# Three quarters of the first MLP product as 2x2 block products with seven products of sums, in a decoder step on one core

## The chip, the core and the metric

The kernel runs on one core of one Trainium2 chip. The metric is the device time of one execution in microseconds, the median of several runs. The engines are TensorE (PE in the profile; its weight loads are PEld), VectorE (DVE), ScalarE (ACT), GpSimd (POOL) and SyncE (SP), which issues all transfers here. Each engine works through its own queue in order and waits on semaphores for the others.

## The reference

One layer of a decoder, for 512 prompt tokens and 8 new tokens (520 columns in all), d_model 1024, hidden size 4096. Two recurrent branches and their merge come first, per-layer inputs and a final norm last. What the change touches is the MLP between them:

```
hm = rms_norm(r, norm_mlp_g)
r = r + jnp.square(jax.nn.relu(hm @ w_ff1)) @ w_ff2      # w_ff1: 1024 x 4096, w_ff2: 4096 x 1024
...
hp = rms_norm(r, norm_ple_g)
r = r + jax.nn.sigmoid(hp @ w_ple_gate) * (p_l @ w_ple_proj)
```

## The kernel before

Activations lie with channels on the partitions and the 520 tokens along the free axis, so a block is 128x520. Matmuls run in a rounded 32-bit format; to keep precision, every operand is split into a high part (the value rounded, written by ACT) and a low part (the rest, a DVE subtraction), and a product is three matmuls: high weight by high activation, high by low, low by high. A matmul takes 260 columns, half of the tokens, since 520 don't fit one bank of PSUM; the result of 520 columns takes a tile `m` of two banks, of which there are two. Single banks `s` come from another pool of four.

The work with weights is a list of units. A unit is a piece of 1024x128 weights (8 tiles of 128x128) and what it multiplies: 8 x 3 x 2 = 48 matmuls (`mm`, L176). `seq` is the order in which weights are prepared. `load` brings the next piece into one of three `raw` buffers; `prep` writes its high part `wh` (ACT, L154) and its low part `wl` (DVE, L159) into one of three buffers each, and asks for the next load. `run_unit` first calls `prep` for the unit two steps ahead, then issues its matmuls, then the evaluation of its result. The order of the code is the order in each engine's queue: the schedule is written by hand.

The first MLP product has 32 units, the second 64 half units (a unit there is 8 of 32 hidden blocks). They go by halves: 16 units of the first product fill 16 hidden blocks (`ev_ff1`: on DVE the rectified product times the tokens' reciprocal root, L874, on ACT its square, L875, then high and low part, L527 and L528), and 16 units of the second product use them, two per output block, with one DVE addition per output block (`ev_ff2`, L887). The same again for the second half. The norm's gain is applied to `hm` before the product, the tokens' factor `rstd` after it.

Of the kernel before, what the change touches and what calls it, by code (L numbers as in the profile page):

```python
# [8 lines left out]
F32 = mybir.dt.float32  # L9
# [10 lines left out]
N = T + NB  # L20
# [5 lines left out]
# columns of w_in  # L26
# [10 lines left out]
class Unit:  # L37
    """One pass of weights: a [1024 or 8 tiles of 128, 128] piece and what it multiplies."""
# [7 lines left out]
def decoder_step_kernel(  # L46
# [73 lines left out]
    # ---------------------------------------------------------------- weights  # L120
    raw_of, w_of = {}, {}

    seq = []  # the units in the order in which their weights are prepared
    done = {"load": 0, "prep": 0}
    w_tags = {}

    def load():
        if done["load"] < len(seq):
            u = seq[done["load"]]
            r = rawp.tile([128, 8, 128], F32, tag="raw", name="raw")  # L130
            units[u].load(r)
            raw_of[u] = r
            done["load"] += 1

    def prep(engines=None, apart=False):
        """The next unit's weights in two parts that sum to them; a generator over the pieces,
        engines has for each the one that rounds and the one that subtracts; apart: a pause between them."""
# [4 lines left out]
        done["prep"] += 1  # L142
        r = raw_of.pop(u)
# [37 lines left out]
    def run_groups(u, lo, hi):  # L181
        """The tiles lo..hi of unit u's list; returns the evacuations that are due."""
# [15 lines left out]
    def run_unit(u):  # L198
        prep_all()
        if u in extra:  # L200
            prep_all()
        due = run_groups(u, 0, 4)
# [6 lines left out]
        w_of.pop(u)  # L209

# [3 lines left out]
    # ------------------------------------------------ phase 0: x, norms, tables  # L214
# [3 lines left out]
    og = {}  # HGRN2's outputs: the pairs 0..2; the last pair, and with it the first head's of retention  # L218
# [63 lines left out]
    def hg_near(p):  # L282
        """Scores of s == t, and of the pairs of neighbours that start at an even token."""
# [16 lines left out]
    def hg_scores(p, lvl):  # L300
        """Scores of the pairs whose level, the half size of their block, is lvl."""
# [38 lines left out]
    def hg_update(p, m):  # L340
        """From the products within blocks of m to those within blocks of 2m."""
# [40 lines left out]
    def v_dec(vT):  # L382
        """The new tokens' values by token, out to memory so that they can be read for all partitions."""
# [38 lines left out]
    def o_dec(q, Sd, psd):  # L422
        """psd rows: for each (g, half) a block of 32 rows, the last 8 of them the new tokens."""
# [8 lines left out]
    def o_ext(psd):  # L432
# [3 lines left out]
        # token 4z+l of group g: column 32(2g+z) + 24 + 4z+l of the l-th block  # L436
# [67 lines left out]
    def rsqrt(out, pieces, scale):  # L504
        """out = (x * scale + EPS) ** -0.5, x given in pieces of out"""
# [7 lines left out]
    def ones_bc(H, L, x=None):  # L513
        """The sum over partitions of H + L (+ x), on every partition: two banks of NH."""
# [58 lines left out]
    # -------------------------------------------------------- retention units  # L573
# [205 lines left out]
    # ------------------------------------------------- merge of the branches  # L779
# [53 lines left out]
    def add_squares(j, r, cs):  # L833
        """The squares of the blocks 0..6, summed, and those of block 7."""
# [28 lines left out]
    # ---------------------------------------------------------------- MLP  # L863
    def ev_ff1(i):
        def ev(ps):
            if i == 0:
                mx["hid"] = pair("X2", "hid")
                a = big.tile([128, 12, N], F32R, tag="B3", name="fa")
                b = big.tile([128, 6, N], F32R, tag="Q", name="fb")
                c = [pair(f"S{i}", "fc", F32R) for i in (0, 1, 2, 4, 5, 6, 7)]  # L870
                mx["f"] = [a[:, k] for k in range(12)] + [b[:, k] for k in range(6)] + \
                    [t[:, k] for t in c for k in range(2)]
# [3 lines left out]
            split(hidH(i % 16), hidL(i % 16), t)  # L876
# [18 lines left out]
    def ff1_half(half):  # L895
        for i in range(16):
            unit(w_ff1[0], (half * 16 + i) * 128, lambda k: mx["hmH"][:, k], lambda k: mx["hmL"][:, k],
                 ev_ff1(half * 16 + i))

    def ff2_half(half):  # L900
        w2 = w_ff2[0].rearrange("(k p) n -> p k n", p=128)
        for j in range(8):
            for z in range(2):
                k0 = half * 16 + z * 8
                src = w2[:, k0:k0 + 8, j * 128:(j + 1) * 128]
# [481 lines left out]
```

## Time and profile before

| | us |
|---|---|
| median of 3 runs | 1116.89 (1116.68 to 1117.96) |
| span of the profiled execution, first to last instruction | 1115.1 |
| PE busy in it | 1104.0 (99%) |
| DVE busy | 568.8 (51%) |
| ACT busy | 418.8 (38%) |
| POOL busy | 25.7 (2%) |
| mean granted TensorE clock | 0.998 |

A row of groups in the profile reads: line, engine, operation, tile written <- tiles read, shapes, count | busy us, mean ns of one | idle time of the engine just before them, and what ended it. A row of the timeline reads: start us, duration us, engine, line, operation, and in brackets the idle time before it with what ended it. A row of windows reads: the stretch, its length, busy us of PE, PEld, DVE, ACT and POOL with the number of instructions, the granted clock, the busy share of the DMA engines and GB/s. A row of waits reads: who waited for whom, us in total, times, the longest.

### The profile page before, as it was taken

How to read it: one execution, taken by the hardware profiler on the slowest of the kernel's cores; microseconds unless marked ns; L12 is line 12 of the kernel's file. 1: busy time of each engine (PE TensorE's matmuls, PEld its weight loads, DVE VectorE, ACT ScalarE, POOL GpSimd, SP SyncE). 2: the span in 40 equal slices, each digit the busy share in tenths (PEclk: the TensorE clock that was granted, in tenths of full speed). 3: DMA queues.
4: the chain of work that ended last, by engine and by line, in shares of the span. 5: the costliest groups of instructions: out<-in, count | busy, mean ns of one | idle time of the engine just before them, and what ended most of it. 6: DMA issues, size and time to landing. Idle time of an engine off the chain costs nothing.

```text
span 1115.1 us, 23376 instructions
## 1 busy us (share of the span) xinstructions
PE 1104.0 (99%) x10433; PEld 1085.7 (97%) x10433; DVE 568.8 (51%) x817; ACT 418.8 (38%) x621; POOL 25.7 (2%) x19
## 2 busy tenths in 40 slices
PE   8999999999999999999999999999999999999997
PEld 8999999999999999999999999999999999999997
DVE  6576767859555754442342554444222344344465
ACT  7223534343344425422322344433112433332365
POOL 1000000000011011000000000000000000000001
PEclk9999999999999999999999999999999999999999
DMA  7535252533445365433323233333333233334302
GB/s 220 152 96 171 82 172 78 156 101 115 136 139 157 114 173 155 119 95 95 95 81 108 78 96 89 104 92 95 96 96 95 76 95 95 95 92 125 88 19 78
DMA packets 231028, 123.03 MB, mean 110 GB/s; under 512 B 3960, under 2 KB 229504, under 8 KB 230800
## 3 DMA queue, kind: packets, MB, share of 16 engines
q1 hardware_dynamic: 230928, 121.54, 37.7%
q8 instruction: 82, 1.34, 0.5%
q14 instruction: 18, 0.15, 0.0%
HBM read 109.89 MB, written 11.63 MB: 109 GB/s over the span
## 4 chain that ended last, share of the span: by engine, by line
PE 98%; DVE 1%; ACT 0%; DMA 0%; issue 0%; SPq 0%; DVEq 0%
PE m L176 83%; PE m L1115 2%; PE s L1115 2%; PE s L309 1%; PE s L428 1%; PE s L489 1%; PE s L711 1%; PE s L465 1%; PE s L668 1%; PE s L491 0%; PE s L713 0%; PE s L292 0%; PE s L452 0%; PE s L404 0%; DMA xn<-in_x_prompt_dram 0%; PE s L617 0%
## 5 line engine op out<-in xcount | busy, mean ns | idle before, releaser
L159 DVE TENSOR_TENSOR wl<-raw,wh 128x1024 fp32r<-128x1024 f32 (+1 forms) x165 | 200.8, 1218 | 186.9 <-ACT wh L154 186.4
L176 PE MATMUL m<-hH,wh 128*128 128x260 f32 x1120 | 231.0, 287 | 0.0
L176 PE MATMUL m<-hH,wl 128*128 128x260 f32 x1120 | 226.0, 283 | 0.0
L176 PE MATMUL m<-hL,wh 128*128 128x260 f32 x1120 | 225.2, 283 | 0.0
L154 ACT ACTIVATE wh<-raw 128x1024 fp32r<-128x1024 f32 (+1 forms) x165 | 172.4, 1046 | 139.1 <-PE m L176 119.7
L176 PEld LDWEIGHTS m<-hH,wh 128*128 128x128 f32 x1120 | 172.3, 188 | 3.4 <-issue 1.7
L176 PEld LDWEIGHTS m<-hH,wl 128*128 128x128 f32 x1120 | 172.6, 188 | 0.0
L176 PEld LDWEIGHTS m<-hL,wh 128*128 128x128 f32 x1120 | 172.5, 188 | 0.0
L176 PE MATMUL m<-hmH,wh 128*128 128x260 f32 x512 | 103.3, 283 | 0.0
L176 PE MATMUL m<-hmH,wl 128*128 128x260 f32 x512 | 103.2, 283 | 0.0
L176 PE MATMUL m<-hmL,wh 128*128 128x260 f32 x512 | 103.0, 283 | 0.0
L176 PE MATMUL m<-fc,wh 128*128 128x260 f32 x448 | 90.1, 282 | 0.0
L176 PEld LDWEIGHTS m<-hmH,wh 128*128 128x128 f32 x512 | 79.0, 188 | 0.1
L176 PEld LDWEIGHTS m<-hmH,wl 128*128 128x128 f32 x512 | 78.9, 188 | 0.0
L176 PEld LDWEIGHTS m<-hmL,wh 128*128 128x128 f32 x512 | 78.7, 188 | 0.0
L176 PE MATMUL m<-fa,wh 128*128 128x260 f32 x384 | 77.2, 282 | 0.0
L176 PE MATMUL m<-fa,wl 128*128 128x260 f32 x384 | 77.1, 282 | 0.0
L176 PEld LDWEIGHTS m<-fc,wh 128*128 128x128 f32 x448 | 69.2, 188 | 0.0
L875 ACT ACTIVATE hid<-hid 128x520 f32<-128x520 f32 x32 | 20.4, 638 | 112.0 <-DVE hid L874 112.0
L176 PEld LDWEIGHTS m<-fa,wl 128*128 128x128 f32 x384 | 59.2, 188 | 0.0
L176 PEld LDWEIGHTS m<-fa,wh 128*128 128x128 f32 x384 | 58.9, 188 | 0.0
L874 DVE SCALAR_TENSOR_TENSOR hid<-m,x 128x520 f32<-128x520 f32 x32 | 22.4, 700 | 51.5 <-PE m L176 51.5
(321 smaller groups left out, 1662.1 us busy)
## 6 DMA issues: line engine op xcount, KB each, us to landing
raw<-in_w_in_dram SPq DMA_DIRECT2D x72, 512.0 KB, 3.9
raw<-in_w_ff_dram SPq DMA_DIRECT2D x64, 512.0 KB, 4.1
vbc<-vdd SPq DMA_DIRECT2D x16, 512.0 KB, 5.4
Sd<-in_state_hgrn_dram SPq DMA_DIRECT2D x8, 512.0 KB
out_dram<-Sd SPq DMA_DIRECT2D x8, 512.0 KB, 5.5
rSd<-in_state_ret_dram SPq DMA_DIRECT2D x8, 512.0 KB, 6.1
out_dram<-rSd SPq DMA_DIRECT2D x8, 512.0 KB
raw<-in_w_up_hg_dram SPq DMA_DIRECT2D x8, 512.0 KB, 3.9
```

What stands on the lines that cost most here:

```text
L154: S.activation(wh[:, k], r[:, k], AF.Copy)
L159: e1.tensor_sub(wl[:, k], r[:, k], wh[:, k])
L176: PE.matmul(ps[:, z, :NH], lhsT=a[:, k, :], rhs=b[:, z * NH:(z + 1) * NH], start=first and i == 0, stop=last and i == 2)
L309: PE.matmul(b[32 * j:32 * j + 32, 32 * hc:32 * hc + 32], lhsT=kx[:, h, o:o + 32], rhs=qx[:, h, o:o + 32], start=True, stop=True)
L428: PE.matmul(b[32 * i:32 * i + 32, :], lhsT=q[g], rhs=Sd[g][:, 4 * z:4 * z + 4, :], start=True, stop=True)
L465: PE.matmul(b[:, c * 128:(c + 1) * 128], lhsT=kn[:, h, c, :], rhs=vn[:, h, c, :], start=True, stop=True)
L489: PE.matmul(o, lhsT=vn[:, h, c, :], rhs=A[:, h * 4 + c, :], start=True, stop=c == 0)
L668: PE.matmul(b[:, c * 256:(c + 1) * 256], lhsT=kn[:, 2 * i + c, :], rhs=vn[:, 2 * i + c, :], start=True, stop=True)
L711: PE.matmul(b[:, cs], lhsT=vn[:, c, zs], rhs=A[:, cs], start=True, stop=c == 0)
L874: V.scalar_tensor_tensor(h2(t), in0=ps, scalar=0.0, in1=h2(mx["rstd"]), op0=ALU.max, op1=ALU.mult)
L875: S.activation(t, t, AF.Square)
L1115: PE.matmul(ps, lhsT=w[:, k, :], rhs=x, start=k == 0 and n == 0, stop=k == 7 and n == 2)
```

## The change

The first 8 units of the first product stay as they are. The other 24 become 12 pairs. A pair's result, two hidden blocks by 520 tokens, is seen as a 2x2 block product: the activations by token half (0 to 259, 260 to 519) and contraction half (blocks 0 to 3, 4 to 7), the weights by contraction half and unit. It is computed with seven half products of 12 matmuls each (4 blocks, three matmuls) instead of eight, from sums and differences of the activations' quarters (`combine_a`, `combine_b`, made once while the first 8 units run; there `rstd` is multiplied in first, by POOL) and of the weights (`prep_pair`, for each pair). The MLP goes by quarters of 8 hidden blocks instead of halves of 16; so the second product has an addition on DVE after each unit instead of after every second one, and the hidden blocks need half the memory, which the sums take.

```diff
+    def prep_pair(n, i):
+        a, b = raw_of.get((n, "a")), raw_of.get((n, "b"))
...
+        def cut(h, src):
+            S.activation(wh[:, 4 * h:4 * h + 4], src, AF.Copy)
+            V.tensor_sub(wl[:, 4 * h:4 * h + 4], src, wh[:, 4 * h:4 * h + 4])
+        c0, c1 = slice(0, 128), slice(128, 256)
+        if i == 0:
+            V.tensor_tensor(u1, a[:, :, c0], a[:, :, c1], op=ALU.add)
+            cut(0, a[:, :, c0])
+            cut(1, u1)
+        elif i == 1:
+            V.tensor_tensor(t2, u1, b[:, :, c1], op=ALU.add)
+            cut(0, t2)
+            V.tensor_tensor(t3, a[:, :, c1], b[:, :, c1], op=ALU.add)
+            load()
+            cut(1, b[:, :, c0])
+        elif i == 2:
+            cut(0, b[:, :, c1])
+            V.tensor_tensor(t2, t2, b[:, :, c0], op=ALU.add)
+            load()
+            cut(1, t3)
+        else:
+            cut(0, t2)
...
+    def combine_a(kp):
...
+            for h in range(2):
+                j = kp + 4 * h
+                S.activation(n[:, h], xT[:, j], AF.Copy, scale=cv[:, V_MLP + j:V_MLP + j + 1])
+                G.tensor_tensor(n[:, h], n[:, h], mx["rstd"], op=ALU.mult)
+            for c, h, z in (("A11", 0, z0), ("A12", 1, z0), ("A22", 1, z1)):
+                H, L = comb[c]
+                split(H[:, kp], L[:, kp], n[:, h, z])
+    def combine_b(kp):
...
+            V.tensor_tensor(t[:, 0], a21, a22, op=ALU.subtract)
+            V.tensor_tensor(t[:, 2], a11, a21, op=ALU.subtract)
+            V.tensor_tensor(t[:, 1], t[:, 0], a11, op=ALU.subtract)
+            V.tensor_tensor(t[:, 3], t[:, 1], a12, op=ALU.add)
+            for i in range(4):
+                H, L = comb[OPERANDS[3 + i]]
+                split(H[:, kp], L[:, kp], t[:, i])
...
+    r1, r2, r5 = (cst[:, 1024 + NH * i:1024 + NH * (i + 1)] for i in range(3))
+    def finish(slot, t):
+        G.tensor_scalar(t, t, 0.0, None, op0=ALU.max)
+        S.activation(t, t, AF.Square)
+        split(hidH(slot), hidL(slot), t)
+    def last_product(n, ps):
+        t = mx["hid"][:, 0]
+        product(n, 3, 0, "A22", ps[:, 0, 0:NH], False)
+        S.activation(t[:, z1], ps[:, 0, 0:NH], AF.Copy)
+        finish(2 * (n % 4), t)
+    def run_quarter(q, then):
...
+        for n in range(4 * q - 4, 4 * q):
+            ps = pm.tile([128, 2, 512], F32, tag="m", name="m")
+            X, Z = ps[:, 0, 0:NH], ps[:, 1, 0:NH]
+            t1, t2 = mx["hid"][:, 0], mx["hid"][:, 1]
+            prep_all()
+            product(n, 0, 0, "A11", X, True)
+            S.activation(r1, X, AF.Copy)
+            product(n, 0, 1, "S1", Z, True)
+            S.activation(r5, Z, AF.Copy)
+            if before is not None:
+                prep_all()
+                last_product(*before)
+            prep_all()
+            product(n, 1, 0, "S2", X, False)
+            S.activation(r2, X, AF.Copy)
+            Y = bank()[:, 0:NH]
+            product(n, 1, 1, "A12", Y, True)
+            V.tensor_tensor(t1[:, z0], r1, Y, op=ALU.add)
+            prep_all()
+            product(n, 2, 0, "S4", Z, False)
+            V.tensor_tensor(t2[:, z0], Z, r2, op=ALU.subtract)
+            product(n, 2, 1, "S3", X, False)
+            V.tensor_tensor(t2[:, z1], r5, X, op=ALU.subtract)
+            finish(2 * (n % 4) + 1, t2)
+            before = n, ps
+        run_unit(then, lambda: last_product(*before))
```

In the text the products of a pair are counted in the order in which they stand here: first A11, second S1, third S2, fourth A12 (into a bank `s`), fifth S4, sixth S3, seventh A22, which is issued behind the next pair's second product. The seven products' line in the changed kernel is L1010, the copies of r1, r5 and r2 are L1037, L1039 and L1045, the DVE subtractions from the accumulators L1051 and L1053, POOL's rectification L1016, the square L1017, the high and low part of a hidden block L588 and L589, the weight sums L167, L171, L173 and L178, the roundings of the weights L162 and their low parts L163, the copy of the seventh product L1024.

**TensorE, between two units or products.** Before, at the border of two units of the first product (`m_` with a number is an accumulator of two banks, `hmH` and `hmL` the activations' high and low part, `wh` and `wl` a unit's weights; in brackets, whose semaphores the instruction waits for):

```order
L176 MATMUL m_7985<-hmH_7351,wh_7861 128x260 x2
L176 MATMUL m_7985<-hmL_7352,wh_7861 128x260 x2
L176 MATMUL m_7985<-hmH_7351,wl_7862 128x260 x2
L176 MATMUL m_8044<-hmH_7351,wh_7920 128x260 [waits DVE_49,Activation_49]
L176 MATMUL m_8044<-hmH_7351,wh_7920 128x260
L176 MATMUL m_8044<-hmL_7352,wh_7920 128x260 x2
L176 MATMUL m_8044<-hmH_7351,wl_7921 128x260 x2
```

A new unit there waits for its accumulator, which an evaluation two units ago has freed, and for its weights. Now, at the border of the first and the second product of the pair whose accumulator is `m_8934`, and then of the seventh product of the pair before (into `m_8830`) and the third of this one (`comb` are the activations' sums, A11 is 7885 and 7886, S1 7891 and 7892, S2 7893 and 7894, A22 7889 and 7890):

```order
L1010 MATMUL m_8934<-comb_7886,wh_8866 128x260
L1010 MATMUL m_8934<-comb_7885,wl_8867 128x260
L1010 MATMUL m_8934<-comb_7891,wh_8866 128x260 [waits Activation_49]
L1010 MATMUL m_8934<-comb_7892,wh_8866 128x260
L1010 MATMUL m_8934<-comb_7891,wl_8867 128x260
```
```order
L1010 MATMUL m_8830<-comb_7889,wl_8901 128x260
L1010 MATMUL m_8934<-comb_7893,wh_8935 128x260 [waits Activation_49]
L1010 MATMUL m_8934<-comb_7894,wh_8935 128x260
L1010 MATMUL m_8934<-comb_7893,wl_8936 128x260 [waits DVE_49]
L1010 MATMUL m_8934<-comb_7893,wh_8935 128x260
```

Within a pair the products go on in the accumulator in use, and each that follows a copy out of it waits for an ACT or DVE instruction. The semaphore values in the build name them: the second product waits for L1037 of its own pair, the third for L1039, the fifth for L1045, the sixth for L1051 and the seventh for L1053.

**ACT.** Before, for each unit of the first product, the square, the high part and the rounding of the weights two units ahead:

```order
L875 ACTIVATE hid<-hid 128x520 [waits DVE_49]
L527 ACTIVATE fa<-hid 128x520 [waits Activation_49]
L154 ACTIVATE wh<-raw 128x1024 [waits DMAHW1_49,PE_49]
L875 ACTIVATE hid<-hid 128x520 [waits DVE_49]
L527 ACTIVATE fa<-hid 128x520 [waits Activation_49]
L154 ACTIVATE wh<-raw 128x1024 [waits DMAHW2_49,PE_49]
```

Now, two stretches of one pair. The first runs from the second hidden block of the pair before to the copies r1 and r5 (`cst` holds the weight sums and the copies), the second from the seventh product of the pair before to the copy r2:

```order
L1017 ACTIVATE hid<-hid 128x520 [waits Pool_49]
L588 ACTIVATE fa<-hid 128x520 [waits Activation_49]
L162 ACTIVATE wh<-cst 128x512 [waits DVE_49,PE_49]
L162 ACTIVATE wh<-rawp 128x512 [waits DMAHW5_49]
L1037 ACTIVATE cst<-m 128x260 [waits PE_49]
L1039 ACTIVATE cst<-m 128x260 [waits PE_49]
```
```order
L1024 ACTIVATE hid<-m 128x260 [waits PE_49]
L1017 ACTIVATE hid<-hid 128x520 [waits Pool_49]
L588 ACTIVATE fa<-hid 128x520 [waits Activation_49]
L162 ACTIVATE wh<-rawp 128x512 [waits DMAHW6_49]
L162 ACTIVATE wh<-cst 128x512 [waits DVE_49]
L1045 ACTIVATE cst<-m 128x260 [waits PE_49]
```

The copies that TensorE waits for stand behind the square, which waits for POOL, and behind roundings of weight sums, which wait for DVE.

**DVE.** Before, three instructions per unit of the first product:

```order
L874 SCALAR_TENSOR_TENSOR hid<-m,x_7811 128x520 [waits PE_49]
L528 TENSOR_TENSOR fb<-hid,fa 128x520 [waits DVE_49,Activation_49]
L159 TENSOR_TENSOR wl<-raw,wh 128x1024 [waits DMAHW2_49,Activation_49]
L874 SCALAR_TENSOR_TENSOR hid<-m,x_7811 128x520 [waits PE_49]
L528 TENSOR_TENSOR fc<-hid,fa 128x520 [waits DVE_49,Activation_49]
L159 TENSOR_TENSOR wl<-raw,wh 128x1024 [waits DMAHW3_49,Activation_49]
```

Now, in one pair, from the low part of the second hidden block of the pair before to the subtractions from this pair's accumulator:

```order
L589 TENSOR_TENSOR fa<-hid,fa 128x520 [waits DVE_49,Activation_49]
L171 TENSOR_TENSOR cst<-cst,rawp 128x512 [waits DMAHW3_49]
L163 TENSOR_TENSOR wl<-cst,wh 128x512 [waits Activation_49]
L173 TENSOR_TENSOR x_7811<-rawp 128x512
L163 TENSOR_TENSOR wl<-rawp,wh 128x512 [waits Activation_49]
```
```order
L178 TENSOR_TENSOR cst<-cst,rawp 128x512 [waits DVE_49]
L163 TENSOR_TENSOR wl<-x_7811,wh 128x512 [waits Activation_49]
L589 TENSOR_TENSOR fa<-hid,fa 128x520 [waits Activation_49]
L167 TENSOR_TENSOR cst<-rawp 128x512 [waits DMAHW4_49]
L163 TENSOR_TENSOR wl<-rawp,wh 128x512 [waits PE_49,Activation_49]
L163 TENSOR_TENSOR wl<-cst,wh 128x512 [waits Activation_49]
L1048 TENSOR_TENSOR hid<-cst,s 128x260 [waits PE_49]
L163 TENSOR_TENSOR wl<-cst,wh 128x512 [waits Activation_49]
L1051 TENSOR_TENSOR hid<-m,cst 128x260 [waits PE_49]
L1053 TENSOR_TENSOR hid<-cst,m 128x260 [waits PE_49]
```

The weight sums L171 and L167 stand behind the low parts of hidden blocks, L589, and these wait for ACT.

More of the change, by code (lines that the diff above doesn't have):

```diff
@@ L142, in prep @@
         done["prep"] += 1
+        if not isinstance(u, int):
+            prep_pair(*u)
+            return
         r = raw_of.pop(u)
@@ L201, in run_unit @@
             prep_all()
-        due = run_groups(u, 0, 4)
+        lo = 0
+        if mid is not None:
+            lo = 3 if len(units[u].groups) == 1 else 2
+            for e, ps in run_groups(u, 0, lo):
+                e(ps[:, :, :NH])
+            mid()
+        due = run_groups(u, lo, 4)
         for f in at.pop(u, []):
@@ L209, in run_unit @@
         w_of.pop(u)
+        if mid is not None:
+            prep_all()
     def unit(w, c, H, L, evac):
@@ L861, in norm_rstd, with hid_slots @@
         rsqrt(mx["rstd"], bs, 1.0 / D)
+    def hid_slots():
+        a = big.tile([128, 12, N], F32R, tag="B3", name="fa")
+        b = big.tile([128, 6, N], F32R, tag="Q", name="fb")
+        mx["f"] = [a[:, k] for k in range(12)] + [b[:, k] for k in range(4)]
     def ev_ff1(i):
@@ L867, in ev @@
                 mx["hid"] = pair("X2", "hid")
[L868 to L872, printed above, removed]
+                hid_slots()
             t = mx["hid"][:, i % 2]
@@ L893, in ev_ff2, with ff2_quarter @@
         return ev
[L895 to L900, printed above, removed]
+    def ff2_quarter(q):
         w2 = w_ff2[0].rearrange("(k p) n -> p k n", p=128)
+        order = (0, 1, 2, 3, 4, 5, 7, 6) if q else range(8)
         for j in range(8):
-            for z in range(2):
-                k0 = half * 16 + z * 8
-                src = w2[:, k0:k0 + 8, j * 128:(j + 1) * 128]
-                slots = [(k, lambda k=k, z=z: (hidH(8 * z + k), hidL(8 * z + k))) for k in range(8)]
-                units.append(Unit(lambda r, s=src: dma(r, s),
-                                  [(slots, z == 0, z == 1, ev_ff2(half, j) if z else None)]))
@@ L910, in p_load @@
-    def p_load():
-        t = big.tile([128, 4, 256], F32, tag="S12", name="pn")
-        dma(t, p_prompt[0, 0].rearrange("(c p) d -> p c d", p=128))
-        t2 = big.tile([8, 256], F32, tag="S13", name="psn")
-        dma(t2, p_sample[0, :, 0])
-        mx["pn"], mx["psn"] = t, t2
+            src = w2[:, q * 8:q * 8 + 8, j * 128:(j + 1) * 128]
+            slots = [(k, lambda k=k: (hidH(k), hidL(k))) for k in order]
+            units.append(Unit(lambda r, s=src: dma(r, s), [(slots, True, True, ev_ff2(q, j))]))
@@ new lines, in decoder_step_kernel, with go @@
+    CTAGS = ("S8", "S9", "S10", "S11", "S12", "S13", "S14", "S15", "S0", "S1", "S2", "S4", "S5", "S6")
+    OPERANDS = ("A11", "A12", "A22", "S1", "S2", "S3", "S4")
+    z0, z1 = slice(0, NH), slice(NH, N)
+    def combine_a(kp):
+        def go():
+            if kp == 0:
+                for i, c in enumerate(OPERANDS):
+                    comb[c] = tuple(big.tile([128, 4, NH], F32R, tag=CTAGS[7 * z + i], name="comb") for z in range(2))
+            n = comb["n"] = pair("S7", "hn")
+            for h in range(2):
[5 more added lines that the diff above has]
+                split(H[:, kp], L[:, kp], n[:, h, z])
+        return go
@@ new lines, in product @@
+    def product(n, i, half, operand, out, start):
+        wh, wl = w_of[n, i]
+        H, L = comb[operand]
+        for k in range(4):
+            for m, (w, x) in enumerate(((wh, H), (wh, L), (wl, H))):
+                PE.matmul(out, lhsT=w[:, 4 * half + k, :], rhs=x[:, k, :], start=start and k == 0 and m == 0,
+                          stop=k == 3 and m == 2, skip_group_check=not start)
+    r1, r2, r5 = (cst[:, 1024 + NH * i:1024 + NH * (i + 1)] for i in range(3))
[3 more added lines that the diff above has]
+        split(hidH(slot), hidL(slot), t)
@@ L939, in ev_proj @@
         return ev
+    flow = list(range(2, len(units)))
     u_ff = len(units)
@@ L957, in decoder_step_kernel @@
         units.append(Unit(ld, groups))
-    ff1_half(1)
-    ff2_half(1)
+    ff2_quarter(3)
+    pair_seq(3, u_proj)
+    flow += [("q", 3, u_proj), *range(u_proj + 1, len(units))]
     HALF = ((256, N), (0, 256))
@@ L1316, in decoder_step_kernel @@
     at[3].append(lambda: late(3))
-    for u in range(2, u_ple):
-        run_unit(u)
+    for u in flow:
+        if isinstance(u, int):
+            run_unit(u)
+        else:
+            run_quarter(*u[1:])
     run_ple()
```

95 lines of the change are left out of this document (80 added, 15 removed).

## The prediction

> **What bounds the kernel now.** I read the page's busy line and chain first, then what TensorE waited for, then the stretch of the two MLP products, then the rows of single operations.
>
> ```profile
> span 1115.1 us, 23376 instructions
> PE 1104.0 (99%) x10433; PEld 1085.7 (97%) x10433; DVE 568.8 (51%) x817; ACT 418.8 (38%) x621; POOL 25.7 (2%) x19
> PE 98%; DVE 1%; ACT 0%; DMA 0%; issue 0%; SPq 0%; DVEq 0%
> ```
>
> The chain that ended last is TensorE's own instruction stream. Its waits are these, and in the stretch of the MLP (second fence) it is never idle:
>
> ```profile
> PE m L1207 <- DMA xs<-in_x_sample_dram: 3.3, 1, 3.3
> PE m L1029 <- DVE sqs L1001: 0.9, 1, 0.9
> PE s L1191 <- DVE xhat L1172: 0.5, 1, 0.5
> ```
> ```profile
> 678.00:1058.50 380.50, 380.50 (x3167) 380.00 (x3166) 149.74 (x165) 125.42 (x162) 0.00 (x0) 1.00 0.34 96
> ```
>
> The second columns of that row are busy time of PE, PEld, DVE, ACT and POOL; then the granted clock, 1.00. So a matmul taken out is time taken out as long as the other engines keep out of TensorE's way. One unit of the first MLP product, engine by engine (start, duration, operation):
>
> ```profile
> 737.12 0.40 PE L176 MATMUL m<-hmH,wl 128*128 128x260 f32 x2
> 737.56 0.70 DVE L874 SCALAR_TENSOR_TENSOR hid<-m,x 128x520 f32<-128x520 f32 x1 [1.51 <-PE m L176]
> 738.30 0.64 ACT L875 ACTIVATE hid<-hid 128x520 f32<-128x520 f32 x1 [3.51 <-DVE hid L874]
> 738.97 0.64 ACT L527 ACTIVATE fa<-hid 128x520 fp32r<-128x520 f32 x1
> 739.51 1.04 ACT L154 ACTIVATE wh<-raw 128x1024 fp32r<-128x1024 f32 x1
> 739.64 0.70 DVE L528 TENSOR_TENSOR fc<-hid,fa 128x520 fp32r<-128x520 f32 x1 [1.37 <-ACT fa L527]
> 740.59 1.23 DVE L159 TENSOR_TENSOR wl<-raw,wh 128x1024 fp32r<-128x1024 f32 x1 [0.25 <-ACT wh L154]
> 743.33 0.70 DVE L874 SCALAR_TENSOR_TENSOR hid<-m,x 128x520 f32<-128x520 f32 x1 [1.52 <-PE m L176]
> ```
>
> From 737.56 to 743.33 is one unit: 5.77 us for 48 matmuls, 0.120 us each. The last matmul of a unit starts at 737.24 and its reader at 737.56, 0.32 later. A hand-over between DVE and ACT takes 0.03 to 0.04 (738.26 to 738.30, 739.61 to 739.64). An ACT operation that does not need the one before starts 0.10 before that one ends (738.97 to 739.51 for a 0.64). All of this chain, 737.56 to 740.34, hides under the next unit's matmuls, because that unit writes another accumulator.
>
> **What the change removes.** Twelve pairs of units cost 96 matmuls each; seven products of 12 make 84. 144 matmuls by 0.120 are 17.3 us off TensorE. Quartering the second product changes no matmul; it adds 16 DVE additions of 0.70 (the 128x520 rows), 5.77 us apart, hidden under TensorE.
>
> **What it adds: four waits of TensorE in each pair.** All products but the fourth accumulate in one two-bank tile, and the sums are copied out between them. The build makes TensorE wait, at the second product, for the ACT copy of the first (L1037), although that product goes to the other bank; at the fifth for the copy r2 (L1045); at the sixth for the DVE subtraction L1051. Each copy stands in its engine's queue behind the preparation of weights two steps ahead, and that behind the evaluation of the pair before. The prices, in mean ns:
>
> ```profile
> L970 DVE TENSOR_TENSOR gt<-m,x 128x264 f32<-128x264 f32 x4 | 1.7, 432 | 3.5 <-PE m L1115 2.0 <-ACT x L511 1.5
> L159 DVE TENSOR_TENSOR wl<-raw,wh 128x512 fp32r<-128x512 f32 x2 | 1.3, 685 | 0.0
> L154 ACT ACTIVATE wh<-raw 128x512 fp32r<-128x512 f32 x2 | 1.1, 614 | 0.0
> L1305 ACT ACTIVATE f<-m 128x264 f32<-128x264 f32 x2 | 0.8, 386 | 0.0
> L156 POOL CAST wh<-raw 128x512 fp32r<-128x512 f32 x2 | 1.2, 611 | 0.0
> L159 POOL TENSOR_TENSOR wl<-raw,wh 128x512 fp32r<-128x512 f32 x2 | 2.5, 1294 | 8.1 <-ACT wh L154 8.1
> L1045 POOL TENSOR_SCALAR yd<-yd,ss 8x1024 f32<-8x1024 f32 x1 | 2.8, 2849 | 651.7 <-ACT ss L511 651.7
> ```
>
> The rectification of 128x520 on POOL has no row. By the CAST row (one input, 128 partitions) it is 0.62; by the TENSOR_SCALAR row, 2.849 x 520/1024, it is 1.45. I take 0.80, nearer the CAST, which has the shape; the other has 8 partitions and a scalar operand. DVE operations of 512 that follow each other start 0.61 apart:
>
> ```profile
> 90.61 0.69 DVE L351 TENSOR_TENSOR qs<-qs,tot 128x512 f32<-128x512 f32 x1 [0.72 <-PE s L332]
> 91.22 0.69 DVE L352 TENSOR_TENSOR kx<-kx,tot 128x512 f32<-128x512 f32 x1
> ```
>
> Wait A, at the second product, from the start of the sixth product's last matmul of the pair before: reader 0.32; DVE subtraction 0.43+0.04; POOL 0.80+0.04; ACT square 0.64+0.03; ACT high part 0.64+0.03; DVE low part 0.61; DVE sum of weights 0.69+0.04; two ACT roundings 0.52 each; ACT copy r1 0.39+0.04. That is 5.78. TensorE has 0.12 and the first product, 12 x 0.120 = 1.44, to run meanwhile: idle 4.22.
>
> Wait B, at the fifth product, from the seventh product of the pair before: 0.32; ACT copy 0.39+0.04; POOL waits for DVE, 0.70 (below); POOL 0.84; square 0.67; high part 0.67; DVE low part 0.61; DVE sum u1 0.69+0.04; ACT rounding 0.52; copy r2 0.43: 5.92. TensorE has 0.12 and two products, 2.88: idle 2.92. In the last pair of a quarter no u1 is made (the next unit's plain rounding, about 0.95, follows the high part's 0.54): 1.88.
>
> Wait C, at the sixth: 0.32 + 0.43 + 0.04 - 0.12 = 0.67.
>
> A quarter's first pair has nothing queued from a pair before: the copies r1 and r5 cost 0.32 + 0.39 + 0.04 - 0.12 = 0.63 each, and C 0.67: 1.93. A quarter is then 1.93 + 2 x (4.22 + 2.92 + 0.67) + (4.22 + 1.88 + 0.67) = 24.3, three quarters 73.0. The unit that takes the last seventh product waits for its last hidden block: 3.67 of evaluation against 3.00 of matmuls left, 0.67, twice; the third time copies of the layer inputs stand in between, about 2 by three more copies of 0.63. Sum 3.3.
>
> The 0.70 in B rests on these rows (POOL's, then DVE's):
>
> ```profile
> 403.25 1.90 POOL L684 TENSOR_TENSOR vbc<-vbc,K 128x1024 f32<-128x1024 f32 x1 [51.11 <-DMA vbc<-vdd]
> 405.34 2.86 POOL L684 TENSOR_TENSOR vbc<-vbc,K 128x1024 f32<-128x1024 f32 x1 [0.19 <-DMA vbc<-vdd]
> ```
> ```profile
> 405.22 1.23 DVE L159 TENSOR_TENSOR wl<-raw,wh 128x1024 fp32r<-128x1024 f32 x1 [0.25 <-ACT wh L154]
> 406.36 2.92 DVE L685 SCALAR_TENSOR_TENSOR rSd<-rSd,vbc 128x1024 f32<-128x1024 f32 x1
> ```
>
> The same POOL operation takes 1.90 alone and 2.86 when it starts inside a DVE operation; the DVE operation behind it takes 2.92. In B, POOL's input is ready while DVE is inside a run of three 512 operations: 0.35 if POOL comes in at the next border, 1.0 if one more DVE operation does. The Trainium skill, "SBUF — State Buffer", section "Who interferes with whom", says that a DVE instruction with two SBUF inputs and a GpSimd instruction that reads SBUF block each other fully, whichever started first holding on. The four rows agree with it. Without that rule the 0.70 falls away nine times, 6.3 us less.
>
> **The preparation stage.** Four steps, each over two of the first eight units, form the sums of the activations. In a step DVE and ACT must do, one after the other: first unit: evaluation 0.74, square 0.67, high part 0.54, rounding of the weights 1.05+0.04, their low part 1.22, two POOL products of 1.31 (the 1294 row; they start after that low part), then 1.18 of high and low parts: 8.1. Second: 0.74 + 0.67 + 0.54 + 1.09 + 1.14 (next DVE start), four differences 1.6, four low parts 1.4: 7.2. That is 15.3 against 11.5 of matmuls, 3.7 too long, 15 over four steps. Some 4.7 of lag fits before the next unit but one needs its accumulator, and part of this comes back when the second product asks for the last hidden block: 10 + 2.8, about 13. Ends: 6, if steps overlap better, and 16.
>
> **The sum.** 73.0 + 3.3 + 13 - 17.3 = +72. Against the profiled execution's own time, 1115.1 of span, that is 1187; the median 1116.89 is 1.8 above this span, so 1189. DVE's throughput alone does not bind: 11 operations of 0.61, three of 0.35 and two of 0.61 are about 9.0 of a pair's 10.1 of matmuls. It is the serial order through four queues that costs.
>
> Ends of the unknowns: POOL 0.62 takes 0.18 off A and B, 3.2 less; 1.45 adds 12. The POOL wait 0.35 or 1.0: 3 less or 3 more. Preparation: 7 less, 3 more. Together 1176 to 1207.
>
> **The rivals.** First, *TensorE's clock drops after the waits* (chance 0.16). Idle stretches of 4.2 us come nine times, longer than the 3.3 at the kernel's start, the longest in this trace. The row of the microsecond after that one shows clock 1.00:
>
> ```profile
> 4.00:5.00 1.00, 1.00 (x8) 0.98 (x8) 0.02 (x1) 0.88 (x4) 0.00 (x0) 1.00 0.65 258
> ```
>
> That speaks against it, though only for one shorter gap. If matmuls ran at half speed, four products of each pair lie on the chain of waits: 48 x 0.120 = 5.8 per pair; in one pair of three +17 (1206), in all nine +52 (1241). The Trainium skill, "TensorE: Matmul & The Clock Gate", section "HAM oscillation — how this bites in real kernels", has the clock halved once an idle gap spans its window of about 3.4 us. No row here has a gap that long in mid-kernel.
>
> Second, *the copies are served at once* (0.07): if the evaluation of the pair before is done before ACT and DVE are asked for r1 and r2, a pair costs 0.63 + 0.67 only. 12 x 1.3 + 3 + 13 - 17.3 = +14: 1131. Against it: one evaluation is 2.8 us long already in the rows from 737.56 on, without POOL or weight sums, while the first product is 1.44.
>
> Third, the other side, *the waits hide* (0.05): TensorE runs seven products without being held. Then only 17.3 counts, less what preparation costs, 0 to 6: 1100 to 1105, faster. It decides when a pair's waits together stay under 1.44 us, the twelve matmuls saved. C and one copy alone are 1.30, so it needs A and B at nearly nothing.
>
> **How the numbers follow.** My forecast has 0.72, 1189. The range 1165 to 1225 takes in its own ends, a little below them for handovers that overlap, and the clock rival up to about six of its nine pairs; what is left out is the second and third rival and the rest of the clock's. Within 0.2% (2.2 us, about what a measurement of this kernel can tell from no change) would need waits of just 17 us in all: 0.01, out of the third rival. Faster 0.04, slower 0.95.
>
> **What would show it.** In the profile after, TensorE's waits should name ACT copies into the constants' array (L1037 about 4 us nine times, L1045 about 3) and the DVE subtraction L1051; PE's busy share in the pair stages should be near 55 to 60%, and a full pair some 18 us long. The matmul count falls by 144. If the waits name POOL's share otherwise, the POOL row's mean tells (0.6 or 1.4). Clock digits below 9 would be the first rival. I am wrong if the second product does not wait for r1, or if ACT reaches r1 within about a microsecond.

## The result: 1238.7 us, and the profile after

The changed kernel takes 1238.67 us (median of four runs, 1237.66 to 1239.98) against 1117.41 before: ratio 1.1085, 95% interval 1.107 to 1.1101. Slower, as forecast, but 49.7 us beyond the 1189 and outside the range. From the page of the changed kernel, the span, the busy line, the row of granted clock in 40 slices, and the head of the chain that ended last:

```profile
span 1238.2 us, 23424 instructions
PE 1143.4 (92%) x10289; PEld 1114.3 (90%) x10289; DVE 651.0 (53%) x997; ACT 473.3 (38%) x765; POOL 73.2 (6%) x51
PEclk9999999999999999999999999878987799679999
PE 82%; ACT 7%; DVE 5%; POOL 4%; issue 2%; DMA 0%; DVEq 0%; SPq 0%; ACTq 0%; POOLq 0%
```

144 matmuls are gone (10433 to 10289), and yet TensorE's busy time rose by 39 us, from 1104.0 to 1143.4: work that is fewer and takes longer points to a lower clock, and the slices from the 26th to the 36th show one. ACT, DVE and POOL, 1% of the chain before, are 16% of it. TensorE's waits that are new (total us, times, longest):

```profile
PE m L1010 <- ACT cst L1037: 39.8, 12, 5.0
PE m L1010 <- ACT cst L1045: 22.2, 9, 3.3
PE m L228 <- DVE hid L939: 6.3, 4, 1.9
PE m L1010 <- DVE hid L1051: 6.3, 12, 0.6
PE m L228 <- ACT fa L588: 4.3, 3, 1.9
PE m L228 <- ACT pj L1086: 3.1, 3, 1.1
PE m L1010 <- ACT cst L1039: 1.4, 3, 0.5
```

These are the waits named in the prediction: A (L1037), B (L1045), C (L1051), the preparation stage (L939 and 1.5 us of L588), the units at the quarters' ends (the rest of L588, and L1086) and the first pairs' r5 (L1039). One wait A in full, from the timeline (start, duration, what; in brackets the idle time before):

```profile
834.43 0.42 DVE L1053 TENSOR_TENSOR hid<-cst,m 128x260 f32<-128x260 f32 x1 [1.81 <-PE m L1010]
834.94 1.51 POOL L1016 TENSOR_SCALAR hid<-hid 128x520 f32<-128x520 f32 x1 [8.16 <-DVE hid L1053]
836.48 0.64 ACT L1017 ACTIVATE hid<-hid 128x520 f32<-128x520 f32 x1 [5.57 <-POOL hid L1016]
837.15 0.64 ACT L588 ACTIVATE fa<-hid 128x520 fp32r<-128x520 f32 x1
837.82 0.70 DVE L589 TENSOR_TENSOR fb<-hid,fa 128x520 fp32r<-128x520 f32 x1 [2.96 <-ACT fa L588]
838.44 0.68 DVE L171 TENSOR_TENSOR cst<-cst,rawp 128x512 f32<-128x512 f32 x1
839.21 0.63 ACT L162 ACTIVATE wh<-cst 128x512 fp32r<-128x512 f32 x1 [1.43 <-DVE cst L171]
839.75 0.61 ACT L162 ACTIVATE wh<-rawp 128x512 fp32r<-128x512 f32 x1
840.27 0.37 ACT L1037 ACTIVATE cst<-m 128x260 f32<-128x260 f32 x1
840.69 0.80 PE L1010 MATMUL m<-comb,wh 128*128 128x260 f32 x2 [4.85 <-ACT cst L1037]
```

It is the chain of the prediction, link by link, except POOL's 1.51 for 0.80. The last row shows the second cause: the first two matmuls behind this wait take 0.80, where the same two behind a wait at full clock take 0.51 (row at 832.68 further below).

### The profile page after: what moved, and what is told of

It reads as the page before. It is cut to its first block, busy times and chain, and to the rows that moved or that the text cites. A ratio compares the mean times of both kernels' runs of the same rounds, so it can differ in the third digit from the quotient of the medians.

```text
span 1238.2 us, 23424 instructions
## 1 busy us (share of the span) xinstructions
PE 1143.4 (92%) x10289; PEld 1114.3 (90%) x10289; DVE 651.0 (53%) x997; ACT 473.3 (38%) x765; POOL 73.2 (6%) x51
## 3 DMA queue, kind: packets, MB, share of 16 engines
q8 instruction: 80, 1.31, 0.4%
## 4 chain that ended last, share of the span: by engine, by line
PE 82%; ACT 7%; DVE 5%; POOL 4%; issue 2%; DMA 0%; DVEq 0%; SPq 0%; ACTq 0%; POOLq 0%
PE m L228 59%; PE m L1010 9%; POOL hid L1016 3%; PE m L1297 2%; PE s L1297 2%; ACT hid L1017 1%; ACT wh L206 1%; ACT wh L162 1%; ACT fa L588 1%; POOL hn L984 1%; PE s L370 1%; PE s L489 1%; DVE comb L589 1%; PE s L526 1%; PE s L772 1%
## 5 line engine op out<-in xcount | busy, mean ns | idle before, releaser
L1010 PE MATMUL m<-comb,wh 128*128 128x260 f32 x576 | 144.1, 350 | 69.7 <-ACT cst L1037 39.8
L1010 PEld LDWEIGHTS m<-comb,wh 128*128 128x128 f32 x576 | 117.8, 249 | 78.1 <-ACT cst L1037 42.6
L228 PE MATMUL m<-fa,wh 128*128 128x260 f32 x768 | 136.1, 286 | 6.2 <-ACT fa L588 4.3
L228 PEld LDWEIGHTS m<-fa,wh 128*128 128x128 f32 x768 | 111.6, 192 | 7.0 <-ACT fa L588 4.9
L228 PE MATMUL m<-fa,wl 128*128 128x260 f32 x512 | 103.9, 285 | 0.0
L1010 PE MATMUL m<-comb,wl 128*128 128x260 f32 x288 | 98.0, 340 | 0.0
L1010 PEld LDWEIGHTS m<-comb,wl 128*128 128x128 f32 x288 | 72.1, 250 | 0.0
L1016 POOL TENSOR_SCALAR hid<-hid 128x520 f32<-128x520 f32 x24 | 38.4, 1600 | 355.5 <-DVE hid L1053 256.9
L1017 ACT ACTIVATE hid<-hid 128x520 f32<-128x520 f32 x24 | 15.3, 638 | 99.8 <-POOL hid L1016 99.8
L228 PE MATMUL m<-fb,wh 128*128 128x260 f32 x256 | 51.6, 283 | 0.7 <-DVE fb L589 0.7
L228 PEld LDWEIGHTS m<-fb,wh 128*128 128x128 f32 x256 | 39.4, 188 | 1.3 <-DVE fb L589 1.3
L163 DVE TENSOR_TENSOR wl<-rawp,wh 128x512 fp32r<-128x512 f32 x36 | 24.7, 687 | 29.9 <-ACT wh L162 29.9
```

The lines of the kernel that those rows point to most:

```text
L163: V.tensor_sub(wl[:, 4 * h:4 * h + 4], src, wh[:, 4 * h:4 * h + 4])
L228: PE.matmul(ps[:, z, :NH], lhsT=a[:, k, :], rhs=b[:, z * NH:(z + 1) * NH], start=first and i == 0, stop=last and i == 2)
L1010: PE.matmul(out, lhsT=w[:, 4 * half + k, :], rhs=x[:, k, :], start=start and k == 0 and m == 0, stop=k == 3 and m == 2, skip_group_check=n ...
L1016: G.tensor_scalar(t, t, 0.0, None, op0=ALU.max)
L1017: S.activation(t, t, AF.Square)
```

## Experiments

The ratios compare with the kernel before, run beside on the same chip (1116.9 to 1118.1). That kernel's own times lie up to 1.1 us apart between the chips, so a difference of about a microsecond between two changed versions says nothing. Names in the diffs: P1, P5, P6, P2, P3, P7 are a pair's products in the order in which they run (the first to the sixth), P4 is its seventh, run inside the next pair.

**Is it the clock?** Filler matmuls of 128x260 into a spare accumulator bank, ahead of the second and the fifth product; nobody reads them.

```diff
             S.activation(r1, X, AF.Copy)
+            if before is not None:
+                fill(n, 0, 38)
...
             prep_all()
+            if before is not None:
+                fill(n, 1, 24)
             product(n, 2, 0, "S4", Z, False)
```

> The changed kernel with filler matmuls that compute nothing used: in each pair but a quarter's first, 38 matmuls of 128x260 (4.6 us) ahead of the second product and 24 (2.9 us) ahead of the fifth, into an accumulator bank that nobody reads, so that TensorE works through waits A and B instead of standing still. Theory 'lower clock': the half-clock spells after the idle gaps cost 20 to 35 of the 121 us, the clock stays near 1.00 and the time falls to 1203 to 1222. Rival 'the chain alone': the waits are set by the other engines, the clock costs next to nothing, and the time stays at 1237 or rises by the few fillers that run over, to 1237 to 1250.

Measured 1213.14 (ratio 1.0853, 1.0837 to 1.0869): 25.5 us less than the changed kernel with 558 matmuls more. The same stretch of three pairs in the changed kernel and then with fillers (the columns are busy us of PE, PEld, DVE, ACT, POOL, then the granted clock):

```profile
778.00:843.00 65.00, 43.65 (x269) 41.50 (x268) 28.52 (x48) 22.14 (x43) 7.54 (x5) 0.81 0.17 50
```
```profile
778.00:843.00 65.00, 61.27 (x491) 59.20 (x490) 33.66 (x54) 26.77 (x52) 9.60 (x6) 1.00 0.20 60
```

0.81 became 1.00, and the time is inside what the theory of the lower clock gave, outside the rival's. So at least 25.5 us are clock; 95.7 remain with TensorE kept busy, and those are the chain. At least, because the fillers ahead of the fifth product outlast the copy r2 by 0.8 us in the last pair of each quarter, 2.4 in all, and three spells of half clock (10.2 us) are left.

**How long must a wait be to cost clock?** Stretches around the first waits of the changed kernel, cut where its clock changes (steps of 3.41 us); the counts behind PE are matmuls:

```profile
695.70:699.12 3.42, 1.56 (x14) 1.39 (x13) 2.44 (x4) 1.38 (x4) 1.30 (x2) 1.00 0.54 151
699.12:702.53 3.41, 3.41 (x17) 3.41 (x18) 2.05 (x3) 2.00 (x3) 0.00 (x0) 0.50 0.00 0
702.53:705.94 3.41, 3.41 (x30) 3.41 (x30) 3.30 (x9) 1.51 (x5) 0.00 (x0) 1.00 0.53 154
712.77:716.18 3.41, 2.33 (x19) 2.36 (x20) 1.79 (x4) 2.23 (x3) 0.00 (x0) 1.00 0.02 5
716.18:719.60 3.42, 3.42 (x31) 3.42 (x29) 3.39 (x8) 1.46 (x4) 0.00 (x0) 1.00 0.35 92
726.42:729.84 3.42, 1.54 (x13) 1.37 (x12) 1.95 (x4) 1.94 (x5) 0.28 (x1) 1.00 0.26 78
729.84:733.25 3.41, 3.41 (x18) 3.41 (x17) 3.03 (x6) 1.52 (x4) 0.00 (x0) 0.50 0.03 6
```

A step of this grid with a single idle stretch of 1.9 us in it (busy 1.56 of 3.42) is followed by a step at half clock; one with busy 2.33 is not. Over the whole traces of all fourteen kernels, from the first record of the clock on and counting each matmul as 0.125 us (0.25 at half clock), 71 steps at full clock were followed by half clock, leaving out the last such step of each kernel; TensorE was at work for 0.43 of each of them or less, and every step with 0.44 or more was followed by full clock (between 0.40 and 0.43 both occur). The clock came back after a step with more than about three quarters of work (between 0.73 and 0.78 both occur). At a kernel's end this count does not hold: in eight of the fourteen a last step with 0.54 to 0.64 by the same count was still followed by half clock. There the matmuls have 1 to 256 columns, not 260 (in the kernel before 16 of 1 and 128 columns); whether that is the reason, no run shows. The Trainium skill, "TensorE: Matmul & The Clock Gate", section "Part 1: The HAM clock gate (the "warmup" mystery)", has a free-running window of 3413 ns, which the spells agree with (3.41, 6.83 or 10.24 us long); the rule of an idle gap above about 3.4 us, in "HAM oscillation — how this bites in real kernels", the rows above contradict: 1.9 us did it, and the shortest such stretch in the changed kernel was 1.75. A test of the two, with 10 fillers ahead of the second product only:

```diff
-                fill(n, 0, 38)
+                fill(n, 0, 10)
...
-                fill(n, 1, 24)
+                fill(n, 1, 0)
```

> As the first kernel with fillers, but only 10 filler matmuls (1.2 us) ahead of the second product and none ahead of the fifth: TensorE's idle stretches at wait A shrink from about 4.4 (up to 5.0) to about 3.2, at wait B they stay at 2.5 to 3.3, so none reaches 3.4 us. Theory 'the share of a fixed stretch': the clock is halved for the next 3.41 us whenever TensorE works less than about 0.42 of a fixed 3.41 us stretch (read from the four traces so far); idle of 2 us or more is enough, most pairs still fall to half clock, and the time is 1224 to 1240. Rival 'a gap as long as the stretch': without an idle stretch of 3.4 us the clock stays at 1.00 as with the full fillers, and the time is 1210 to 1218.

Measured 1232.45 (ratio 1.1031): the waits at L1037's place were 31.5 us in 12, the longest 3.8, so six idle stretches exceeded 3.4, against the plan; but 17 spells of half clock remained, 88.7 us (18 and 109.2 in the changed kernel, 3 and 10.2 with full fillers; the spell at each kernel's end is not counted), and 11 of the 17 follow a step whose idle stretch was only 1.9 to 3.2 us long. So no stretch of 3.4 us is needed; the share of the step tells them apart, but for the band from 0.40 to 0.43.

**POOL.**

```diff
     def finish(slot, t):
-        G.tensor_scalar(t, t, 0.0, None, op0=ALU.max)
+        V.tensor_scalar(t, t, 0.0, None, op0=ALU.max)
```

> The changed kernel with the rectification in finish (L1016) on DVE instead of POOL, nothing else. Theory 'POOL is on the chain': its 1.51 us and the wait for DVE before it leave the chain of both A and B, a DVE operation of about 0.5 comes in: about 1.2 us less 18 times and less half clock, 1200 to 1218. Rival 'the queues set it': DVE is as late with one operation more in its queue as POOL was, and the time stays within 1228 to 1245.

Measured 1206.60 (ratio 1.0792, 1.0776 to 1.0808), 32.1 less. The same with fillers (28 and 15), to take the clock out:

```diff
+        V.tensor_scalar(t, t, 0.0, None, op0=ALU.max)
...
+                fill(n, 0, 28)
...
+                fill(n, 1, 15)
```

> The run with the rectification on DVE, with filler matmuls that compute nothing used in its waits (28 ahead of the second product, 15 ahead of the fifth), so that the clock stays up as in the first run with fillers. It prices POOL's rectification without the clock. Theory 'POOL was on the chain twice a pair': the difference to the first run with fillers (1213.1) is 18 times 1.2 to 1.5 us, 22 to 27 us, and the time 1186 to 1192. Rival 'most of the 32 us that the move to DVE gave was clock': the difference is 12 us or less, and the time 1201 or more.

Measured 1189.03 (1.0641, 1.0625 to 1.0657): 24.1 less than the 1213.14, as the theory gave, but not where it said. The copies r1 of the first quarter with fillers, POOL first, then DVE:

```profile
779.14 0.39 ACT L1044 ACTIVATE cst<-m 128x260 f32<-128x260 f32 x1 [0.47 <-PE m L1010]
794.51 0.37 ACT L1044 ACTIVATE cst<-m 128x260 f32<-128x260 f32 x1
813.79 0.37 ACT L1044 ACTIVATE cst<-m 128x260 f32<-128x260 f32 x1
833.06 0.37 ACT L1044 ACTIVATE cst<-m 128x260 f32<-128x260 f32 x1
```
```profile
779.26 0.39 ACT L1044 ACTIVATE cst<-m 128x260 f32<-128x260 f32 x1 [0.47 <-PE m L1010]
793.42 0.37 ACT L1044 ACTIVATE cst<-m 128x260 f32<-128x260 f32 x1
811.14 0.37 ACT L1044 ACTIVATE cst<-m 128x260 f32<-128x260 f32 x1
828.85 0.37 ACT L1044 ACTIVATE cst<-m 128x260 f32<-128x260 f32 x1
```

A full pair, from the second to the third copy and from the third to the fourth, is 19.27 us with POOL at full clock and 17.71 without: 1.56 less, where two passes of 1.2 to 1.5 would be 2.4 to 3.0. From the first copy to the second, where of the two only wait A lies, it is 1.2 less (1.1 in the other two quarters). So the move pays some 1.1 us at A and only 0.4 at B: six times 1.56 and three times 1.1 to 1.2 make 12.8 us. The other half falls behind the last copy r1 of each quarter. There both hidden blocks of the last pair were rectified on POOL one after the other, and the waits of the units are 5.3 us shorter without it; and 2.0 us are the fillers themselves, because 24 ahead of the fifth product outlast the copy r2 of the last pair by 0.8 us and 15 by 0.1. That the total came out as expected is in part luck.

**The tile-wide wait.**

```diff
-            X, Z = ps[:, 0, 0:NH], ps[:, 1, 0:NH]
+            X, Z = ps[:, 0, 0:NH], bank()[:, 0:NH]
```

> The changed kernel with Z in an accumulator tile of its own instead of the second bank of X's tile, so that the second product no longer waits for the copy r1 of X. Theory 'the tile-wide wait': the copy then has two products (2.9 us) more of cover, wait A falls from 4.4 to about 1.5 a pair, and the time to 1190 to 1212. Rival 'the wait moves': the third product, which writes X, waits as long as the second did, and the time stays within 1228 to 1242.

Measured 1173.26 (ratio 1.0498, 1.0483 to 1.0514), 65.4 less, more than expected. Its waits:

```profile
PE m L1010 <- ACT cst L1037: 16.9, 9, 2.1
PE m L1010 <- ACT cst L1045: 15.4, 9, 2.8
PE m L228 <- ACT fa L588: 7.6, 3, 3.0
```

A fell by 22.9 and B by 6.8; C (6.3) and the first pairs' 1.4 are gone too, which I had not counted. Ten spells of half clock are left, 34.1 us, though no wait after the kernel's start is longer than 3.0.

**The control: quarters without block products.** 32 plain units in quarters of 8, no sums of activations; the projection's two units stay behind the last quarter's first product.

```diff
-            u = len(units)
+            u = len(units) + 8
+            ff1_quarter(q)
             ff2_quarter(q)
-            pair_seq(q, u)
...
-            flow += [("q", q, u), *range(u + 1, u + 8)]
...
+            flow += range(u - 8, u + 8)
```

> The changed kernel's order in quarters of 8 hidden blocks, but with all 32 units of the first MLP product as plain units, no sums of activations and no block products (the full product with the matmuls of the kernel before). All theories: the quarters themselves cost nothing, 1115 to 1121; 16 more DVE additions lie under TensorE. If it is above 1125, the quarters are a cause of their own.

Measured 1118.77 (ratio 1.0009, 0.9999 to 1.0018): the quarters cost nothing that this measurement can tell, 2 us at most.

**The order.** Weight preparation is cut into single operations (p; o opens the next step), and the evaluation of a hidden block into its own (q the rectified square, h the high part, l the low part; 1 and 2 the two blocks). C21 is the copy of the seventh product, t1a is the DVE addition to the fourth, t2a and t2b are the DVE subtractions from the accumulators. The changed kernel's order and the new one, for all engines at once, as lists of these tokens:

```diff
-o pppppp P1 r1 P5 r5 o pppppp P4 C21 q1 h1 l1 o pppppp P6 r2 P2 t1a o pppppp P3 t2a P7 t2b q2 h2 l2
+o p p p p q2 p P1 h2 P5 o r1 p p l2 p p P4 p C21 r5 p p p q1 o p p h1 P6 r2 P2 o p l1 p p t1a P3 t2a p p P7 t2b p
```

> The changed kernel with another order of ACT's and DVE's work in a pair (the preparation of weights cut into single operations; the evaluation of a pair's second hidden block after the next pair's first product; copies ahead of preparation that can wait), but with Z still in X's tile and the rectification still on POOL. Theory 'serial chain plus tile-wide wait': order alone recovers part only, 25 to 40 us, to 1190 to 1215, and the second product still waits for r1. Rival 'the queues alone': with the copies served at once a pair costs 1.3 us, and the time falls below 1150.

Measured 1162.82 (ratio 1.0404, 1.0388 to 1.0419): 75.9 less, between the times that the two theories gave. The waits of the products:

```profile
PE m L1016 <- ACT cst L1055: 15.0, 12, 1.4
PE m L1016 <- DVE hid L1058: 7.3, 12, 0.7
PE m L1016 <- ACT cst L1056: 5.5, 9, 0.9
```

L1055 is the copy r5, L1058 the subtraction of wait C, L1056 the copy r2. No wait for r1 is left, against the first theory; the largest here is 1.4, for r5, which reads Z, by a product that writes X: the tile again. I had under-counted the clock, which comes back with the short waits (mean 0.991 after 0.955).

**All parts together.** Own bank, rectification and square in one DVE operation, combining without POOL and spread over eleven units; first in the old order, then in the new one (the token lines above; the single operations of a weight preparation stand in the same order in both, which is slightly other than in the changed kernel).

```diff
-        G.tensor_scalar(t, t, 0.0, None, op0=ALU.max)
-        S.activation(t, t, AF.Square)
...
+            "q": lambda: V.scalar_tensor_tensor(t, in0=t, scalar=0.0, in1=t, op0=ALU.max, op1=ALU.mult),
...
-                S.activation(n[:, h], xT[:, j], AF.Copy, scale=cv[:, V_MLP + j:V_MLP + j + 1])
-                G.tensor_tensor(n[:, h], n[:, h], mx["rstd"], op=ALU.mult)
+                V.scalar_tensor_tensor(n[:, h], in0=xT[:, j], scalar=cv[:, V_MLP + j:V_MLP + j + 1], in1=mx["rstd"],
+                                       op0=ALU.mult, op1=ALU.mult)
...
-        at[u_ff + 1 + (2 * kp * 7) // 8].append(combine_a(kp))
-        at[u_ff + 1 + ((2 * kp + 1) * 7) // 8].append(combine_b(kp))
+        at[u_ff + (1, 3, 6, 9)[kp]].append(combine_a(kp))
+        at[u_ff + (2, 5, 8, 11)[kp]].append(combine_b(kp))
```

> The changed kernel with Z in its own bank, rectification and square in one DVE operation (no POOL, no ACT square), the combining steps without POOL (gain and norm in one DVE operation) and spread over eleven units instead of eight, in the order of the changed kernel. Theory: TensorE's waits fall to about 20 us in the MLP, and little half clock is left: 1116 to 1128. Rival 'DVE becomes the bound' (about 10 us of DVE for 10.1 of matmuls a pair): waits of 3 us a pair remain, 1140 or more.

> The kernel with the parts of the run before (own bank, DVE evaluation, combining spread) and the new order of ACT's and DVE's work in a pair. Theory: no wait over 1.3 us remains, some 4 us in all, and the 144 matmuls taken out come through: 1101 to 1110. Rival 'DVE becomes the bound': DVE is over 95% busy in the pairs, the order changes little, and the time is within 5 us of the run before.

Measured 1120.10 (ratio 1.002, 1.0011 to 1.003) in the old order and 1101.02 (0.9853, 0.9837 to 0.987) in the new: a version 1.5% faster than the kernel before. In the old order one wait of a pair is left, for the copy r2 (11.6 us in nine). In the new order, the busy line and three pairs:

```profile
PE 1086.3 (99%) x10289; PEld 1067.7 (97%) x10289; DVE 663.4 (60%) x1029; ACT 452.2 (41%) x733; POOL 23.7 (2%) x19
```
```profile
853.00:883.00 30.00, 30.00 (x254) 30.00 (x253) 27.02 (x49) 16.93 (x35) 0.00 (x0) 1.00 0.29 88
```

TensorE is never idle there, DVE 90% busy and still not in the way. Against the 1117.79 beside it this is -16.8, of 17.3 that the 144 matmuls are worth. Then each part was taken back alone: Z into `ps[:, 1, 0:NH]`; rectification on POOL and square on ACT; the combining as in the changed kernel.

```diff
-            X, Z, Y = ps[:, 0, 0:NH], bank()[:, 0:NH], bank()[:, 0:NH]
+            X, Z, Y = ps[:, 0, 0:NH], ps[:, 1, 0:NH], bank()[:, 0:NH]
```
```diff
-            "q": lambda: V.scalar_tensor_tensor(t, in0=t, scalar=0.0, in1=t, op0=ALU.max, op1=ALU.mult),
+            "q": lambda: (G.tensor_scalar(t, t, 0.0, None, op0=ALU.max), S.activation(t, t, AF.Square)),
```
```diff
+                S.activation(n[:, h], xT[:, j], AF.Copy, scale=cv[:, V_MLP + j:V_MLP + j + 1])
+                G.tensor_tensor(n[:, h], n[:, h], mx["rstd"], op=ALU.mult)
...
+        at[u_ff + (1, 2, 4, 6)[kp]].append(combine_a(kp))
+        at[u_ff + (1, 3, 5, 7)[kp]].append(combine_b(kp))
```

> The best kernel so far (1101.0) with Z back in the second bank of X's tile and nothing else changed. Theory 'the wait goes by the tile': every product that follows a copy out of the tile waits for it, 0.3 to 0.9 us about two times a pair, and the time is 1115 to 1128. Rival 'the order alone hides it': within 3 us of 1101.

> The best kernel so far with the rectification back on POOL and the square on ACT (two operations for one on DVE), nothing else changed. Theory 'POOL is on the chain': 1.5 us of POOL, its waits for DVE, and ACT held behind it bring waits of 1 to 2.7 us back, 30 to 50 us, 1130 to 1155. Rival 'with the new order it is off the chain': 1101 to 1110.

> The best kernel so far with the combining steps as the changed kernel has them (gain on ACT, norm on POOL, over the first eight units), nothing else changed. Theory: the waits of the preparation stage (6.3 us in the changed kernel) and what they push past its end come back, with one or two spells of half clock: 1108 to 1118. Rival 'hidden': within 3 us of 1101.

Measured 1123.78 (ratio 1.0057) with the shared tile, 1129.12 (1.0111) with POOL and ACT's square, 1114.25 (0.9975) with the old combining: +22.8, +28.1 and +13.2 over the 1101.02. The second is just below what was expected, the others inside; each of the three parts is needed. Shared tile:

```profile
PE m L1016 <- ACT cst L1055: 9.3, 12, 1.0
PE m L1016 <- DVE hid L1058: 6.4, 12, 0.6
```

That is 15.7 us in 12 pairs, 1.31 a pair.

POOL's row with the new order (count, busy us and mean ns), 1.84 us for one rectification:

```profile
L1023 POOL TENSOR_SCALAR hid<-hid 128x520 f32<-128x520 f32 x24 | 44.1, 1836 | 524.4 <-ACT wh L161 334.1 <-DVE hid L1059 154.7 <-ACT hid L1032 35.6
```

## Why the prediction was right in sign and wrong in size

**The removal** (17.3): right. The best version gets 16.8 of it.

**The first rival, the clock, is the step that failed.** It was given 0.16, the forecast assumed 1.00, and the clock cost at least 25.5 us, half of the miss. I set it aside by the row of 4 to 5 us in the kernel before, clock 1.00 after 3.3 us of idling. That reading was wrong. The same transposes in that trace, there and later:

```profile
4.26 1.97 PE L1196 MATMUL m<-cid 128*128 128x128 f32 x8
11.24 0.60 PE L1196 MATMUL m<-cid 128*128 128x128 f32 x4
```

Eight from 4.26 to 6.18, 0.24 each; four from 11.24 to 11.68, 0.11 each. By these equal matmuls the clock was at half there; the trace's first record of the clock comes at 7.6 us, and ahead of it the column shows 1.00 without one. The measure that I went by (idle stretches of 4.2 us against 3.3) was the wrong one as well: stretches of 1.75 and 1.9 us were followed by half clock. Fewer matmuls ran at half speed than in the rival's worst case (+52), because a step with enough work brings the clock back.

**Wait A** (4.22 of idle, nine times): the mechanism was right. Measured 39.8, of which about 1.4 in the three first pairs, so 4.3 each, but beside products that ran partly at half clock; where the products ran at full clock it is 4.85 to 4.95 (four of the nine), and with fillers 38 of them (4.6) and 0.3 more. The excess is POOL's 1.51 against 0.80. I chose the CAST row as the nearest; the other end, the TENSOR_SCALAR row with 8 partitions scaled by its length, 1.45, was the better guide.

**Wait B** (2.92, in a quarter's last pair 1.88: 23.2 in nine): 22.2. The size is right, but in part by luck: POOL's price was too low and its wait for DVE (0.70 every time) too high, and they nearly cancel. That wait shows as a longer POOL operation:

```profile
L1016 POOL TENSOR_SCALAR hid<-hid 128x520 f32<-128x520 f32 x24 | 38.4, 1600 | 355.5 <-DVE hid L1053 256.9 <-ACT hid L1024 98.6
```

Of the 24, 19 take 1.51 and five 1.78 to 2.27; a mean of 1.60 leaves 2.2 us for waiting on DVE in all, where 6.3 were written. For 18 passes the prediction had 14.4 + 6.3 = 20.7, measured are 18 x 1.60 = 28.8: an estimated 8 us of the miss.

**Wait C** (0.67): 6.3 in 12, 0.53. What I left out is the restart: after a wait the first two matmuls take 0.51 instead of 0.40, also at full clock:

```profile
832.68 0.51 PE L1010 MATMUL m<-comb,wh 128*128 128x260 f32 x2 [0.52 <-DVE hid L1051]
833.14 0.40 PE L1010 MATMUL m<-comb,wh 128*128 128x260 f32 x2
```

With three to four waits in each of 12 pairs, 0.11 each is an estimated 4 to 5 us.

**A full pair** was to be some 18 us long: it is 19.27 at full clock (with fillers), and 21.5 to 23.6 in the changed kernel.

**The preparation stage** (13): the four waits of L939, 6.3, and what the first units of the second MLP product wait for the last hidden block, 1.5 + 0.2: 8.0, near the lower end that I gave; the steps overlap better than I summed. **The units at the quarters' ends** (3.3): L588 and L589 2.8 + 0.5, L1086 3.1, together 6.4; both hidden blocks of the last pair pass POOL one after the other there, and I counted one.

Together: 25.5 clock, 8 POOL, 4 to 5 restarts, 3.1 quarter ends, minus 5.0 preparation, make 36 of 49.7. The run with fillers still has 10.2 us of half clock, worth up to 5, and 2.4 us of fillers that ran over; both would be clock too. Some 6 us or more I cannot place by a run.

**The second and third rival** (copies served at once; waits hide) did not happen in this kernel, but the new order shows that they can: the third's condition, waits below what the matmuls save, holds in the best version. Its argument that C and one copy alone come to 1.30 a pair held only while Z shared X's tile: in the new order with the shared tile the waits are those 1.31 a pair, the second rival's price, and with Z in a tile of its own they are gone.

## What to carry to other kernels

In this kernel, trading matmuls for additions paid only once the serial chain was off TensorE's path. So give each accumulator that is read midway a tile of its own, keep slow engines off the chain, and interleave the evaluation with the next products in each queue; here each of these alone left the kernel slower than before (1173, 1207, 1163 us), and together, with the combining steps spread, they gave nearly all that the removed matmuls are worth. Price idle time of TensorE twice: as a wait, and as the half clock that followed here when matmuls of 260 columns filled less than about 0.43 of a 3.41 us step. To see the clock, compare the durations of equal matmuls; do not rely on the clock column where the trace has no record yet.

## Unexpected in the hardware

After a wait of 1.9 us TensorE's clock was at half for 3.41 us (rows above). POOL needs 1.51 us for a rectification of 128x520 that DVE does in 0.43 (the run with the rectification on DVE), and 2.85 for the TENSOR_SCALAR of 8x1024: 2.9 and 2.8 ns for each element of a row, with 128 partitions and with 8, so in these two rows the time goes by the length of a row. A CAST of 128x512 took POOL only 0.61, so the operation counts as much as the shape. A stream of matmuls that resumes after a wait lost about 0.11 us here.
